# Fifteen products that nobody reads, behind the last product of a two-layer encoder

## The chip, the cores and the metric

The kernel runs on one core of a Trainium2 chip. The metric is the device time of one execution in microseconds (us); less is better. Inputs and outputs lie in the chip's memory, and everything between is one launch.

## The reference

Two encoder layers on 256 tokens of width 1024, all in fp32. In short:

```python
for l in range(2):
    # mixer: one projection to 2560 columns, three groups of attention heads side by side
    proj = rms_norm(x, norm1_g[l]) @ w_in[l]
    out_a = neighbourhood_attention(...)      # 4 heads
    out_d = dilated_window_attention(...)     # 6 heads
    out_c = gqa_block_attention(...)          # 6 heads
    x = x + concat(rms_norm each group) @ w_out[l]
    # feed-forward, 2816 wide
    g, u = split(rms_norm(x, norm2_g[l]) @ w_gate_up[l], 2)
    g = depthwise_conv_centred(g, conv_w[l], conv_b[l])
    x = x + (gelu(g) * u) @ w_down[l]
return x
```

## The kernel before

Tokens stand in two tiles of 128 partitions. Every weight matrix is streamed from memory in units of at most 1 MB (tile `raw`), and each fp32 number is split into two parts, `hi` (rounded to the type fp32r) and `lo` (the rest), on ACT and DVE. A full-precision product is then written as three fp32r products into one accumulator (`mm3`, line 708: hi·hi, hi·lo, lo·hi; lo·lo is left out). Where the profile's names show `wp_hi`, `wp_lo`, `act_ch`, `act_cl` and so on, they are such parts. TensorE's rows show fp32r and fp32 alike as `f32`.

Products into four banks of the tag `psa` hold long sums (projections, the down projection's `dacc`); four more banks of the tag `psw` hold short ones. Products on fp32 data that is not split occur only as transposes, which go through `nc.tensor.transpose` with the 128x128 identity `ident`. Scores of a pair of heads use row halves of the array: the heads' 64 rows lie on partitions 0 to 63 (`LOW`) and 64 to 127 (`HIGH`), and the products alternate between the two halves and write to two banks. At the kernel's start 28 bf16 products on the tile `warm` fill the wait for the first data. No product on column halves (a 64-column stationary operand that writes 64 partitions) occurs.

What is recorded is not what is issued: every call `nc.tensor...` goes through a planner (class `Plan`), which gives each engine's instructions an order from an estimate of times and, among those that could start at the same time, from a rank. `nc.later(n)` adds n to the rank. All instructions are issued at line 472 (1547 is the end of the program: each engine drains there, and all meet at a barrier), so the profile's rows are told apart by tile names, not by lines.

The end of the program is this. The last layer's last down projection (`down(last)`) completes the four quarters of the output (two token tiles by two halves of the columns), which are sums in the four banks of `psa` (`dacc`). For each quarter DVE scales the sum and adds it to the residual `xs` (SCALAR_TENSOR_TENSOR, output `const_x`), and SP writes it out (`out_dram<-const_x`). One quarter is cut in two, and its columns 768 to 1024 are summed in a bank of their own (`end`, of the tag `psw`). The planner puts the quarter of token tile 0 and columns 0 to 512 last, so the program's last eight products, 512 columns wide, go into its bank. The lines for `end`:

```python
nc.vector.scalar_tensor_tensor(xs[:, 1, hs], hold["end"], r2[:, 1:2], xs[:, 1, hs], ALU.mult, ALU.add)
nc.sync.dma_start(ov[:, 1, hs], xs[:, 1, hs])
```

Of the kernel before, what the change touches and what calls it, by code (L numbers as in the profile page):

```python
# [11 lines left out]
F32 = mybir.dt.float32  # L12
# [6 lines left out]
P = 128  # L19
S = 256  # L20
# [3 lines left out]
HD = 64  # L24
# [214 lines left out]
class Plan:  # L239
# [5 lines left out]
    def pool(self, real, name, bufs, space=bass.MemoryType.SB):  # L245
        return PlanPool(self, real, name, bufs, space)
# [271 lines left out]
def encoder_kernel(  # L518
# [21 lines left out]
    nc = Plan(tc)  # L540
# [8 lines left out]
    psw = pool("psw", 4, space=bass.MemoryType.PSUM)  # L549
# [8 lines left out]
    ident = const.tile([P, P], F32, tag="ident", name="ident")  # L558
# [18 lines left out]
    warm = const.tile([P, P], mybir.dt.bfloat16, tag="warm", name="warm")  # L577
# [168 lines left out]
    def mean_squares(name):  # L746

        ss = small.tile([P, NT, 2], F32, tag="ssx", name=f"ssx_{name}", bufs=2)
        for h in range(2):
            for t in range(NT):  # L750
                junk = act.tile([P, 512], F32, tag="s2k", name=f"sq_{name}{t}{h}", bufs=NS2K)
                nc.scalar.activation(
                    junk, xs[:, t, h * 512 : (h + 1) * 512], AF.Square, accum_out=ss[:, t, h : h + 1]
                )
        s1 = small.tile([P, NT], F32, tag="s1x", name=f"s1_{name}", bufs=2)
        nc.gpsimd.tensor_tensor(s1, ss[:, :, 0], ss[:, :, 1], op=ALU.add)
        me = small.tile([P, NT], F32, tag="mex", name=f"me_{name}", bufs=2)
        nc.gpsimd.tensor_scalar(me, s1, 1.0 / D, EPS, ALU.mult, ALU.add)
        r = small.tile([P, NT], F32, tag="rx", name=f"rx_{name}", bufs=2)
        nc.gpsimd.tensor_tensor(r, me, minus_half[:, :NT], op=ALU.pow)  # L760
        return me, r
# [127 lines left out]
    for l in range(DEPTH):  # L889
# [68 lines left out]
        if l == 0:  # L958
# [3 lines left out]
            gq = const.tile([P, DEPTH * 3 * HD], F32, tag="gq", name="gq")  # L962
# [6 lines left out]
            gq = gq.rearrange("p (l a d) -> p l a d", l=DEPTH, d=HD)  # L969
# [359 lines left out]
        _, r2 = mean_squares(f"n2{l}")  # L1329
# [148 lines left out]
        if l == DEPTH - 1:  # L1478
            hs = slice(768, 1024)
            nc.vector.scalar_tensor_tensor(xs[:, 1, hs], hold["end"], r2[:, 1:2], xs[:, 1, hs], ALU.mult, ALU.add)  # L1480
            nc.sync.dma_start(ov[:, 1, hs], xs[:, 1, hs])
    nc.emit()


# [67 lines left out]
```

## Time and profile before

| | |
|---|---|
| median of three runs | 608.33 us (607.88 to 609.16) |
| the profiled execution, first to last instruction (span) | 606.6 us |
| granted TensorE clock | 1.000 |
| PE busy | 600.9 us, 99% of the span, 3496 products |
| DVE busy | 484.9 us, 80% |
| ACT busy | 428.6 us, 71% |
| POOL busy | 80.9 us, 13% |

The page gives no time of the profiled execution beside its span. The median of the runs lies 1.7 us above that span; what lies around the first and the last instruction is in that difference. A product's duration in a row runs to its modelled end and overlaps the next product's; how often products follow each other is read from the differences of their starts.

### The profile page before, as it was taken

The numbers are of one execution on the slowest core, as the hardware profiler recorded it, in microseconds if no ns is written. First come the engines' busy times: TensorE is split into PE (matmuls) and PEld (weight loads), VectorE is DVE, ScalarE is ACT, GpSimd is POOL, SyncE is SP. The second block draws the span as 40 slices with busy tenths as digits, with TensorE's granted clock in tenths as the row PEclk, the third lists the DMA queues.
The fourth block names the chain that finished last, engine by engine and source line by source line (L and its number), as shares of the span: only waits on it lengthen the run. The fifth ranks groups of instructions, "written<-read, shape, count | busy, mean of one in ns | idle before, by whom it ended". The sixth has DMA issues, their size and how long they took to land.

```text
span 606.6 us, 9899 instructions
## 1 busy us (share of the span) xinstructions
PE 600.9 (99%) x3496; PEld 526.7 (87%) x3496; DVE 484.9 (80%) x995; ACT 428.6 (71%) x1065; POOL 80.9 (13%) x130
## 2 busy tenths in 40 slices
PE   8999999999999999999999999999999999999997
PEld 7999898888888888888899989888888888888886
DVE  4899897997788988887777898777977777777775
ACT  6889999686666767666688899676765555665661
POOL 2733030103400000000022214421000000000000
PEclk9999999999999999999999999999999999999999
DMA  8994303566598899988455726844465555555601
GB/s 280 296 294 140 105 36 107 195 202 228 185 224 297 278 342 322 318 304 290 153 147 162 248 70 243 291 163 139 142 205 209 174 175 206 184 166 207 199 9 69
DMA packets 85217, 121.44 MB, mean 200 GB/s; under 512 B 9880, under 2 KB 69880, under 8 KB 85168
## 3 DMA queue, kind: packets, MB, share of 16 engines
q1 hardware_dynamic: 82896, 112.17, 56.3%
q0 software_dynamic: 1728, 8.39, 3.9%
q8 instruction: 27, 0.44, 0.3%
q10 hardware_dynamic: 544, 0.26, 0.2%
q14 instruction: 22, 0.18, 0.1%
HBM read 110.93 MB, written 9.88 MB: 199 GB/s over the span
## 4 chain that ended last, share of the span: by engine, by line
PE 96%; ACT 2%; DVE 1%; POOL 0%; issue 0%; DVEq 0%; ACTq 0%; POOLq 0%
PE psw_w L472 53%; PE psa_a L472 43%; ACT act_s2k L472 1%; ACT wp_hi L472 0%; DVE act_z L472 0%; DVE wp_lo L472 0%; POOL small_rstd L472 0%; ACT act_z L472 0%; ACT act_hT L472 0%; DVE act_sw L472 0%; POOL small_ms L472 0%; DVE const_x L472 0%; DVE act_qo L472 0%; POOL const_warm L472 0%; DVEq L472 0%
## 5 line engine op out<-in xcount | busy, mean ns | idle before, releaser
L472 DVE TENSOR_TENSOR wp_lo<-wp_raw,wp_hi 128x512 fp32r<-128x512 f32 (+2 forms) x332 | 231.5, 731 | 59.1 <-ACT wp_hi L472 39.3
L472 ACT CAST wp_hi<-wp_raw 128x512 fp32r<-128x512 f32 (+2 forms) x332 | 203.0, 663 | 22.8 <-PE psw_w L472 10.2
L472 PE MATMUL psw_w<-act_hT,wp_hi 128*128 128x512 f32 x704 | 180.4, 393 | 0.0
L472 PEld LDWEIGHTS psw_w<-act_hT,wp_hi 128*128 128x128 f32 x704 | 127.8, 189 | 24.8 <-DVE act_hT L472 0.7
L472 PE MATMUL psa_a<-wp_hi,act_hT 128*128 128x384 f32 (+2 forms) x448 | 113.1, 333 | 0.7 <-ACT wp_hi L472 0.7
L472 PEld LDWEIGHTS psw_w<-act_hT,wp_lo 128*128 128x128 f32 x704 | 97.7, 190 | 6.8
L472 PE MATMUL psw_w<-act_hT,wp_lo 128*128 128x256 f32 x704 | 102.2, 282 | 0.0
L472 PEld LDWEIGHTS psa_a<-wp_hi,act_hT 128*128 128x128 f32 x448 | 78.3, 189 | 3.4 <-ACT wp_hi L472 0.9
L472 ACT COPY act_s2k<-psw_w 128x256 f32<-128x256 f32 x88 | 32.4, 373 | 62.2 <-PE psw_w L472 61.9
L472 PE MATMUL psa_a<-wp_lo,act_hT 128*128 128x384 f32 (+2 forms) x224 | 74.4, 334 | 0.1
L472 PE MATMUL psa_a<-wp_lo,act_ch 128*128 128x512 f32 (+1 forms) x176 | 68.9, 392 | 0.0
L472 PE MATMUL psa_a<-wp_hi,act_ch 128*128 128x512 f32 x176 | 68.8, 392 | 0.0
L472 PE MATMUL psa_a<-wp_hi,act_cl 128*128 128x512 f32 (+1 forms) x176 | 68.5, 393 | 0.0
L472 DVE TENSOR_TENSOR act_s2k<-psw_w,act_s2k 128x256 f32<-128x256 f32 x88 | 36.6, 421 | 14.5 <-ACT act_s2k L472 14.1
L472 PEld LDWEIGHTS psa_a<-wp_lo,act_hT 128*128 128x128 f32 x224 | 42.2, 189 | 2.4 <-DVE wp_lo L472 1.0
L472 PEld LDWEIGHTS psa_a<-wp_hi,act_cl 128*128 128x128 f32 x176 | 33.1, 188 | 7.5
L472 PEld LDWEIGHTS psa_a<-wp_hi,act_ch 128*128 128x128 f32 x176 | 33.2, 189 | 6.7
L472 PEld LDWEIGHTS psa_a<-wp_lo,act_ch 128*128 128x128 f32 x176 | 33.1, 188 | 6.7
L472 DVE SCALAR_TENSOR_TENSOR act_s2k<-act_s2k,act_cw,act_s2k 128x255 f32<-128x255 f32 x88 | 36.7, 477 | 1.4 <-ACT act_s2k L472 1.3
L472 ACT ACTIVATE act_s2k<-act_s2k 128x512 f32<-128x512 f32 x22 | 13.9, 631 | 30.2 <-DVE act_s2k L472 30.2
L472 ACT ACTIVATE act_s2k<-act_s2k,act_cw 128x256 f32<-128x256 f32 x44 | 24.1, 595 | 15.3 <-DVE act_s2k L472 15.3
L472 POOL TENSOR_TENSOR small_rstd<-small_ms,const_mh 128x6 f32<-128x6 f32 (+2 forms) x26 | 30.8, 1186 | 14.4 <-DVE small_ms L472 12.8
(132 smaller groups left out, 791.6 us busy)
## 6 DMA issues: line engine op xcount, KB each, us to landing
wp_raw<-in_w_gate_up_dram SPq DMA_DIRECT2D x44, 1024.0 KB, 5.1
wp_raw<-in_w_down_dram SPq DMA_DIRECT2D x22, 1024.0 KB, 7.3
wp_raw<-in_w_in_dram SPq DMA_DIRECT2D x14, 768.0 KB, 6.0
wp_raw<-in_w_in_dram SPq DMA_DIRECT2D x8, 1024.0 KB, 9.1
wp_raw<-in_w_out_dram SPq DMA_DIRECT2D x8, 768.0 KB, 8.4
dram_khi<-act_mixT_hi SPq DMA_DIRECT2D x4, 768.0 KB, 3.6
dram_klo<-act_mixT_lo SPq DMA_DIRECT2D x4, 768.0 KB, 8.3
wp_lo<-dram_klo POOLq DMA_DIRECT2D x4, 768.0 KB, 4.8
```

Source lines behind the costliest of these rows:

```text
L472: getattr(o.engine.real, o.method)(*map(real, o.args), **{k: real(v) for k, v in o.kw.items()})
```

## The change

Behind everything else, 15 products are recorded with `later(100000)`. They read finished data (`gq`, the query gains, as fp32; `ident`; `warm`, bf16) and write to banks of `psw` that nobody reads afterwards: six on column halves, two on the full array, four on row halves, all fp32 and 256 columns wide, and three in bf16, 512 wide.

```diff
+    with nc.later(100000):
+        z = psw.tile([P, 512], F32, tag="w", name="idle0")
+        flat = gq.rearrange("p l a d -> p (l a d)")
+        for _ in range(3):
+            for r in (slice(0, HD), slice(HD, P)):
+                nc.tensor.matmul(z[r, :S], ident[:, r], flat[:, :S], start=True, stop=True)
+        z = psw.tile([P, 512], F32, tag="w", name="idle1")
+        for _ in range(2):
+            nc.tensor.matmul(z[:, :S], ident, flat[:, :S], start=True, stop=True)
+        z = [psw.tile([P, 512], F32, tag="w", name=f"idle{i}") for i in (2, 3)]
+        for _ in range(2):
+            for r, y in zip((slice(0, HD), slice(HD, P)), z):
+                nc.tensor.matmul(y[:, :S], ident[r], flat[r, :S], start=True, stop=True)
+        z = psw.tile([P, 512], F32, tag="w", name="idle4")
+        for _ in range(3):
+            nc.tensor.matmul(
+                z.rearrange("p (a b) -> p a b", b=P), warm, warm.unsqueeze(1).to_broadcast([P, 4, P]),
+                start=True, stop=True,
+            )
     nc.emit()
```

TensorE's instructions at the end of the program, before (-) and now (+); `psa_a_157` is the bank of the quarter that is completed last (`dacc[0][0]`), `psw_w_124`, `117`, `166` and `83` are the four banks of `psw`, and the last of these was `end`:

```order
 L472 MATMUL psa_a_157<-wp_lo_248,act_ch_828 128x512
 L472 MATMUL psa_a_157<-wp_hi_240,act_cl_838 128x512
-L1547 UNCONDITIONAL_BRANCH
+L472 MATMUL psw_w_124<-const_gq_178,const_ident_89 64x256 x6
+L472 MATMUL psw_w_117<-const_gq_178,const_ident_89 128x256 x2
+L472 MATMUL psw_w_166<-const_gq_178,const_ident_89 128x256
+L472 MATMUL psw_w_83<-const_gq_178,const_ident_89 128x256
+L472 MATMUL psw_w_166<-const_gq_178,const_ident_89 128x256
+L472 MATMUL psw_w_83<-const_gq_178,const_ident_89 128x256
+L472 LDWEIGHTS const_warm_77
+L472 MATMUL psw_w_124<-const_warm_77 128x512
+L472 LDWEIGHTS const_warm_77
```

All fifteen stand behind the last product of the computation, ahead of TensorE's end of program; two more pairs of a weight load and a bf16 product follow the last row. No row of another engine moves.

## Prediction

> **What bounds the kernel now.** I read the page first, then the chain of work that ended last, then the last microseconds in order of time, then what each engine does at the end of the program, since that is where the new products go.
>
> ```profile
> span 606.6 us, 9899 instructions
> ...
> PE 600.9 (99%) x3496; PEld 526.7 (87%) x3496; DVE 484.9 (80%) x995; ACT 428.6 (71%) x1065; POOL 80.9 (13%) x130
> ...
> PE 96%; ACT 2%; DVE 1%; POOL 0%; issue 0%; DVEq 0%; ACTq 0%; POOLq 0%
> ```
>
> TensorE bounds the kernel: 99% busy, and 96% of the chain that ended last. Work added to it is paid in full, unless it stands where something else ends later. The chain's last pieces (start, length, what) show that place:
>
> ```profile
> 557.99 11.18 PE psw_w L472 x64
> 569.16 5.58 PE psa_a L472 x24
> ...
> 600.86 1.87 PE psa_a L472 x8
> 602.73 0.02 issue
> 602.75 0.75 DVE const_x L472
> ```
>
> In order of time (the first row is DVE's, the rest run in order):
>
> ```profile
> 600.92 0.48 DVE L472 SCALAR_TENSOR_TENSOR const_x<-psw_w,small_rx,const_x 128x256 f32<-128x256 f32 x1
> ...
> 602.08 0.40 PE L472 MATMUL psa_a<-wp_lo,act_ch 128*128 128x512 f32 x1
> 602.32 0.39 PE L472 MATMUL psa_a<-wp_hi,act_cl 128*128 128x512 f32 x1
> 602.75 0.75 DVE L472 SCALAR_TENSOR_TENSOR const_x<-psa_a,small_rx,const_x 128x512 f32<-128x512 f32 x1 [1.35 <-PE psa_a L472]
> 603.53 0.33 SPq L472 DMA_DIRECT2D out_dram<-const_x  x1
> ```
>
> TensorE's last product ends at 602.71; DVE then works until 603.50, and SP issues the last transfer at 603.53. The span ends 3.9 us after TensorE's end, at 606.6. What fills that time stands under the line of the end of the program (for each engine and operation: count, durations min/median/max in ns, first and last start), and in SP's own waits (in total, times, longest):
>
> ```profile
> L1547 SPq EVENT_SEMAPHORE  x9: 27/28/28, 603.9 to 605.7; - x9
> L1547 SPq DRAIN  x2: 7/10/13, 605.8 to 605.9; - x2
> L1547 POOLq EVENT_SEMAPHORE  x2: 17/17/17, 605.9 to 606.0; - x2
> L1547 PEldq DRAIN  x1: 3227/3227/3227, 599.5 to 599.5; - x1
> L1547 DVEq DRAIN  x1: 789/789/789, 602.8 to 602.8; - x1
> ```
>
> ```profile
> SPq L1547 <- DMA out_dram<-const_x: 1.4, 1, 1.4
> ```
>
> Every engine drains and then meets the others. TensorE's drain is taken up early and ends with its last product: 599.5 + 3.23 = 602.7. DVE's ends at 602.8 + 0.79 = 603.6. SP waits 1.4 us for the last transfer to land and drains at 605.9; only then does POOL pass its first semaphore (605.9), which lets all go on. From there to the end of the span it is another 606.6 - 605.9 = 0.7 us of drains and semaphores. So TensorE has 605.9 - 602.7 = 3.2 us in which it may work for nothing; the ends are rounded to a tenth, and I take 3.1. Beyond that, each microsecond is one of the kernel's time.
>
> **The change part by part.** The forecast is therefore one sum, X, the time from the end of the last real product to the end of the last idle one, less 3.1.
>
> *Waits: nothing.* Four of the five idle banks' readers are long done. The bank `end` is read by DVE's addition of 256 columns, which starts at 600.92 and takes 0.48: over at 601.4, before TensorE is through with the real products at 602.7. Behind an idle product on TensorE stands nothing but its drain. DVE's last addition, SP's last transfer and its landing depend on the real product, which ends at 602.71 as before, so none of them moves. All transfers of weights are over.
>
> *The price of a product.* Rows whose starts show how closely products follow each other: 24 products of 512 columns in 5.58 us, 0.23 each; 64 in 11.18, half of them 512 and half 256 wide, leave (11.18 - 32 x 0.23) / 32 = 0.12 for 256 columns. These are fp32r. For bf16, and for the only products on fp32 data that is not split, the transposes, there are their group's row (mean duration 280 ns) and the rows in order of time:
>
> ```profile
> L472 PE MATMUL psw_w<-const_ident,const_x 128*128 128x128 f32 x64 | 9.7, 280 | 0.0
> ```
>
> ```profile
> 6.57 0.82 PE L472 MATMUL psw_w<-const_warm 128*128 128x256 bf16 x6
> 7.30 0.44 PE L472 MATMUL psa_a<-wp_hi,act_hT 128*128 128x384 f32 x1
> 7.58 0.34 PE L472 MATMUL psa_a<-wp_lo,act_hT 128*128 128x384 f32 x1
> 7.76 0.60 PE L472 MATMUL psw_w<-const_ident,const_x 128*128 128x128 f32 x4
> 8.11 0.60 PE L472 MATMUL psa_a<-wp_hi,act_hT 128*128 128x384 f32 x2
> ```
>
> Six bf16 products of 256 columns, 0.82 with the last one's 0.28 (the duration of 256 columns in the row at 47.45 below): (0.82 - 0.28) / 5 = 0.11, so 0.22 for 512 columns and 3 x 0.22 = 0.66 for the three idle ones. Four transposes of 128 columns: (0.60 - 0.28) / 3 = 0.11, twice the price of fp32r per column, though a transpose's price may be that of its weight load.
>
> The fp32 products, twelve of 256 columns, have no row. In the compiled program each stands as two weight loads and two products; TensorE has 27 products more than before (24 and the three in bf16). Lower bound of one such issued product: that of fp32r, 0.12. Upper bound: an fp32 product made whole from two parts of each operand takes four partial products (the kernel's own split takes three and leaves one out), two for each issued one, so 2 x 0.12, or the row of 512 columns, 0.23. The transposes, the nearest row, say 0.22 for 256 columns. I take 0.23.
>
> [...]
>
> *Halves side by side.* The kernel's scores work on row halves:
>
> ```profile
> 45.22 0.34 PE L472 MATMUL psa_a<-wp_hi,act_hT 128*128 128x384 f32 x1
> 45.48 1.70 PE L472 MATMUL psw_w<-act_ko,act_qo 64*128 64x256 f32 x24
> 47.11 0.50 PE L472 MATMUL psa_a<-wp_hi,act_hT 128*128 128x256 f32 x2
> 47.45 0.28 PE L472 MATMUL psa_a<-wp_lo,act_hT 128*128 128x256 f32 x1
> ```
>
> 24 products in 47.11 - 45.48 = 1.63 us, 0.07 each where a full one of that width takes 0.12: the two halves run at the same time. An idle fp32 product issues its two parts on the same half, one after the other; then come the two of the other half. In order of issue only the second part of one product can run beside the first part of the next. Four products on row halves (8 parts) then take 5 turns, six on column halves (12 parts) take 7. For column halves no row exists; bounds are 7 turns, if they behave as row halves do, and 12, if one follows the other. I take 7, by the row of the row halves, the nearest.
>
> *Changing the form.* The burst holds 12 x 0.12 = 1.40 of work in 1.63, and before it lies 45.48 - 45.22 = 0.26 where a product of 384 columns takes 0.17; after it, the second product follows at 47.11 + 0.50 - 0.28 = 47.33, 0.22 instead of 0.12. Together 0.23 + 0.09 + 0.10 = 0.42 for there and back, 0.2 a change. The idle products change four times (full, columns, full, rows, full): 0.8 us.
>
> *The sum:* column halves 7 x 0.23 = 1.61; full 4 x 0.23 = 0.92; row halves 5 x 0.23 = 1.15; bf16 0.66; changes 0.8. X = 5.14. TensorE's drain would end at 602.7 + 5.1 = 607.9 instead of 602.7, 2.0 after the others are ready. Span 606.6 + 2.0 = 608.6. The median of the runs lies 1.7 above the span, so 608.3 + 2.0 = 610.3, slower by 0.33%. A measurement of this kernel can tell about 0.2%, 1.2 us, from no change; X would have to exceed 3.1 + 1.2 = 4.3 for that.
>
> **The rivals.**
>
> *Column halves in series, row halves side by side.* For it: the trace shows no product on column halves. X = 5.14 + 5 x 0.23 = 6.3, cost 3.2, time 611.5. [...]
>
> *Everything in series.* Were the pairing undone by the two parts that follow each other on one half: another 3 x 0.23, X = 7.0, cost 3.9, time 612.2. Against it: the row halves' burst.
>
> *Not slower: a pass of fp32 costs what fp32r costs.* With 0.12 for each issued product and halves side by side, X = 16 x 0.12 + 0.66 + 0.8 = 3.4, cost 0.3, time 608.6; in series 24 x 0.12 + 1.46 = 4.3, cost 1.2, time 609.5, at the edge. It decides if an issued product takes under (4.3 - 1.46) / 16 = 0.18. For it: no row has a whole fp32 product. Against it: the transposes' 0.22.
>
> [...]
>
> *Nothing happens,* or less: the end of the program doesn't wait for TensorE, or the end moves by other means. The drain that ends with the last product speaks against it. Time 608.3. I see no way to a gain.
>
> **How the numbers follow.** Halves side by side at 0.23: 0.45. Column halves in series: 0.20. All in series: 0.13. Fp32 at the price of fp32r: 0.13. Four passes per issued product: 0.05. Nothing: 0.04. The likeliest gives 610.3; with the first three cases lie 0.78 between 610.3 and 612.2. The range takes these in, with 0.4 for noise above and down to 608.9 for the cheaper fp32 in part: 608.9 to 612.6. Slower by over 0.2% are cases one to three and five: 0.83. Within 0.2% are the cheap fp32, which straddles the edge, and nothing: 0.15. Faster: 0.02, for noise.
>
> **What would show it.** In the changed kernel's trace: TensorE's rows go on after 602.3, in five groups, with 12, 4, 8 and 3 products; starts 0.23 apart on the full array; on row halves some pairs of starts a few ns apart; no idle time before the first. TensorE's drain ends at 607.9 and is the last, so POOL's first semaphore follows it and not SP's drain; SP's wait for the transfer stays 1.4; DVE's last addition stays at 602.75. I am wrong if POOL's semaphore stays at 605.9, if starts on the full array are 0.12 or 0.47 apart, or if a real product starts later than before.

## The result and the profile after

The changed kernel took 609.64 us (median of 13 runs, 609.30 to 610.99) against 608.55 (13 runs, 607.88 to 609.37): ratio 1.0018, 95% interval 1.0009 to 1.0026, so 0.5 to 1.6 us slower. The forecast was 610.3 us and 0.33%: the direction is right, the time lies in the range, and the size is about half.

The profiled execution's span went from 606.6 to 608.7, 2.1 us more. That is one execution against one, and not all of it is the change's. The page's first line, and the end of the chain of work that ended last (start, length, what):

```profile
span 608.7 us, 9954 instructions
```

```profile
569.86 5.58 PE psa_a L472 x24
...
601.56 1.85 PE psa_a L472 x8
603.41 4.33 PE psw_w L472 x27
```

The piece `psa_a x8` is the last real one; before it started at 600.86. The real work ended 0.7 us later in this execution, though nothing ahead of it was changed; an earlier piece, of 24 products, stood 0.7 later already (569.86, before 569.16), and the second profile of before, below, is late by 0.6 too. Behind the last real piece stand 27 products, 4.33 us. Before, the chain went on to DVE there; now TensorE itself ends last. In order of time, with TensorE's weight loads (PEld), whose rows separate the forms (column halves, full array, row halves, bf16):

```profile
603.02 0.39 PE L472 MATMUL psa_a<-wp_hi,act_cl 128*128 128x512 f32 x1
603.34 1.06 PEld L472 LDWEIGHTS psw_w<-const_gq,const_ident 128*64 128x64 f32 x12 [0.37 <-issue]
603.34 3.64 PE L472 MATMUL psw_w<-const_gq,const_ident 128*64 128x256 f32 x24
603.45 0.75 DVE L472 SCALAR_TENSOR_TENSOR const_x<-psa_a,small_rx,const_x 128x512 f32<-128x512 f32 x1 [1.35 <-PE psa_a L472]
...
604.79 0.73 PEld L472 LDWEIGHTS psw_w<-const_gq,const_ident 128*128 128x128 f32 x4 [0.39 <-issue]
605.85 0.73 PEld L472 LDWEIGHTS psw_w<-const_gq,const_ident 64*128 64x128 f32 x8 [0.33 <-issue]
606.91 0.33 PEld L472 LDWEIGHTS <-const_warm 128*128 128x128 bf16 x3 [0.33 <-issue]
606.92 0.82 PE L472 MATMUL psw_w<-const_warm 128*128 128x512 bf16 x3
```

Counts of 12, 4, 8 and 3 are as forecast: two loads and two products for each fp32 product. The groups start 603.34, 604.79, 605.85 and 606.92, and the last product ends at 606.92 + 0.82 = 607.74. DVE's last addition follows its product by the same distance as before (its start 603.45 against 603.02; before 602.75 against 602.32). The end of the program, under its line (1567 here), and SP's waits:

```profile
L1567 SPq EVENT_SEMAPHORE  x12: 17/28/1389, 604.6 to 608.6; - x12
L1567 POOLq EVENT_SEMAPHORE  x4: 17/17/17, 608.0 to 608.6; - x4
L1567 SPq DRAIN  x3: 7/7/13, 607.9 to 608.2; - x3
```

```profile
SPq L1567 <- PE psw_w L472: 1.4, 1, 1.4
SPq L1567 <- DMA out_dram<-const_x: 1.3, 1, 1.3
```

One thing here was not forecast. SP passes one semaphore after another at the end; one of them now is TensorE's own, for which SP waits 1.4 us after it has waited 1.3 for the transfer. Only after that come SP's remaining step and its drain (607.9), and POOL's first semaphore at 608.0. So POOL does not follow TensorE's drain at once, but 0.2 us after TensorE's last product. From the last real product's end (603.41) to POOL's first semaphore it is 4.6 us, before 3.2 (605.9 against 602.7): 1.4 us longer, in agreement with the timed 0.5 to 1.6.

### The profile page after: what moved, and what is told of

Read it like the earlier page. It is cut to its first block, busy times and chain, and to the rows that moved or that the text cites. A ratio compares the mean times of both kernels' runs of the same rounds, so it can differ in the third digit from the quotient of the medians.

```text
span 608.7 us, 9954 instructions
## 1 busy us (share of the span) xinstructions
PE 605.1 (99%) x3523; PEld 528.3 (87%) x3523; DVE 484.9 (80%) x995; ACT 428.3 (70%) x1065; POOL 81.0 (13%) x130
## 4 chain that ended last, share of the span: by engine, by line
PE 96%; DMA 1%; ACT 1%; DVE 1%; POOL 1%; issue 0%; SPq 0%
PE psw_w L472 52%; PE psa_a L472 44%; DMA const_x<-in_x_dram 1%; ACT act_s2k L472 0%; SPq L472 0%; POOL small_rstd L472 0%; POOL small_ms L472 0%; DVE act_z L472 0%; ACT act_hT L472 0%; DVE wp_lo L472 0%; DVE act_sw L472 0%; ACT wp_hi L472 0%; POOL const_gq L472 0%; DVE act_qo L472 0%
```

## The experiments

**A second profile of the kernel before** (no edit).

> The kernel before once more, for a second profile. In the two profiles the last real product ended 0.70 us later in the changed kernel than in the one before, though nothing ahead of it was changed. Theory (it is the variation of one execution to the next, from transfers and POOL's waits in the first 40 us): the last real product ends somewhere between 602.5 and 604 here too, and the end behind it is the same 3.2 us. Rival (the change shifts the earlier work): it ends at 602.7 within 0.1.

One execution, 609.06 us, span 607.3. Its chain and its end:

```profile
601.46 1.87 PE psa_a L472 x8
603.33 0.03 issue
603.36 0.75 DVE const_x L472
```

```profile
L1547 SPq DRAIN  x3: 7/7/13, 606.4 to 606.7; - x3
```

The last real product ends at 603.3, 0.6 later than in the first profile of the same kernel, and SP's first drain follows by 3.1 as it did there. The other profiles with untouched real work have their last piece end at 602.7 to 603.2. So the 0.7 us are the variation of executions. It arises far ahead of the change, and not only in the first 40 us as expected: by the starts of TensorE's products, this profile is 0.1 us behind the first one at 390 us and 0.6 at 399 us, the changed kernel's 0.5 and 0.7. What held TensorE there stays open. Comparisons below go from the last real product's end, or by timed ratios.

**A short tail.** The column and row halves are left out (against the changed kernel):

```diff
-        for _ in range(3):
-            for r in (slice(0, HD), slice(HD, P)):
-                nc.tensor.matmul(z[r, :S], ident[:, r], flat[:, :S], start=True, stop=True)
...
-            for r, y in zip((slice(0, HD), slice(HD, P)), z):
-                nc.tensor.matmul(y[:, :S], ident[r], flat[r, :S], start=True, stop=True)
```

> Only the two full fp32 products and the three in bf16 are left behind the last real product: 4 x 0.22 + 3 x 0.22 = 1.5 us of TensorE's time instead of 4.3. Theory (the end of the program waits for the last landing anyway, so about 3 us behind the last product are free): within 0.1% of before, and POOL's first semaphore again follows SP's drain some 3.2 us after the last real product. Rival (idle products cost wherever they stand, since TensorE bounds the kernel): 1.5 us slower, 0.25%. Rival (any idle product at the end makes SP wait for TensorE's own semaphore and so lengthens the end): 0.1 to 0.3 us slower even here.

Ratio 1.0001 (0.9992 to 1.0010). In its chain and under its end of program (line 1559):

```profile
603.20 1.51 PE psw_w L472 x7
```

```profile
L1559 SPq EVENT_SEMAPHORE  x12: 17/28/28, 604.4 to 607.1; - x12
L1559 POOLq EVENT_SEMAPHORE  x4: 17/17/17, 606.4 to 607.0; - x4
```

1.51 us of products cost nothing that the times can tell: POOL's first semaphore comes 606.4 - 603.2 = 3.2 after the real work, as before. That rules out that an idle product costs wherever it stands (0.25%). The smaller lengthening of 0.1 to 0.3 us is too small for the times, but the profile speaks against it: none of SP's steps takes over 28 ns, where one took 1389 in the changed kernel, so TensorE's semaphore is met before SP comes to it.

**Twice as many products of each form.** The four loops run 6, 4, 4 and 6 times:

```diff
-        for _ in range(3):
+        for _ in range(6):
             for r in (slice(0, HD), slice(HD, P)):
...
```

> The same five groups, each with twice as many products, and still four changes of form: TensorE's time behind the last real product is 2 x 3.67 + 0.65 = 8.0 us. Theory (free up to 3.0, then one for one): cost 8.0 - 3.0 = 5.0 us against before, 0.83%; starts stay 0.22 apart. Rival (the cost is mostly in the changes of form, or a fixed one of having idle products): 1 to 2 us, 0.2 to 0.3%. Rival (everything paid): 8.0 us, 1.3%.

Ratio 1.0092 (1.0078 to 1.0106), 4.7 to 6.4 us. Chain, and the starts of the forms:

```profile
603.06 7.99 PE psw_w L472 x54
```

```profile
602.99 2.36 PEld L472 LDWEIGHTS psw_w<-const_gq,const_ident 128*64 128x64 f32 x24 [0.36 <-issue]
...
605.73 1.59 PEld L472 LDWEIGHTS psw_w<-const_gq,const_ident 128*128 128x128 f32 x8 [0.38 <-issue]
607.66 1.60 PEld L472 LDWEIGHTS psw_w<-const_gq,const_ident 64*128 64x128 f32 x16 [0.33 <-issue]
609.58 0.98 PEld L472 LDWEIGHTS <-const_warm 128*128 128x128 bf16 x6 [0.33 <-issue]
```

7.99 - 3.0 = 5.0: beyond the free stretch it is one for one, and neither everything nor a fixed sum is paid. The differences between this kernel and the changed one price each form without its change: full array 1.93 against 1.06, 0.87 for four parts more, 0.22 each; columns 2.74 against 1.45, 1.29 for 12 parts more; rows 1.92 against 1.06, 0.86 for eight. So two parts on halves take one turn of 0.22 (a turn is the time of one issued part). What is left of each group is the change of form: 0.16, 0.19, 0.20, and 0.09 ahead of the first product (603.34 - 603.02 - 0.23), 0.64 in all.

**The same products ahead of the real ones.**

```diff
-    with nc.later(100000):
+    with nc.later(-100000):
```

> The same fifteen products with a rank that puts them ahead of the last 36 or so real products instead of behind the last one; some of those real products change places among themselves. Theory: here nothing covers them, so all of their 4.3 us are paid, 0.7%, and DVE's last addition is 4.3 us later against the start of the last down projection, while the end of the program behind the last real product is as long as before (3.2 us to POOL's first semaphore). Rival (the place makes no difference): 1.1 to 1.4 us, 0.2%, as behind the last product.

The idle products now stand among the last down projection's. Ratio 1.0076 (1.0061 to 1.0092), 3.7 to 5.6 us, which takes in all of the 4.3 us: three to four times what the same products cost behind the last one. The idle products begin at 596.32, and the chain behind them ends thus:

```profile
596.32 3.64 PE L472 MATMUL psw_w<-const_gq,const_ident 128*64 128x256 f32 x24
...
599.90 0.82 PE L472 MATMUL psw_w<-const_warm 128*128 128x512 bf16 x3
```

```profile
569.51 5.58 PE psa_a L472 x24
...
605.52 1.87 PE psa_a L472 x8
607.39 0.03 issue
607.42 0.75 DVE const_x L472
```

DVE's last addition starts at 607.42 instead of 602.75 or, in the second profile of before, 603.36: 4.1 to 4.7 later. Counted from the same piece of 24 products (569.51 here, 569.16 before), it is 37.91 us and was 33.59: 4.3 later. POOL's first semaphore, at 610.6, again comes 3.2 us behind the last real product, at 607.4. The place decides.

**Only one half of each kind.** Products stay as many, but none has another half to run beside:

```diff
-            for r in (slice(0, HD), slice(HD, P)):
+            for r in (slice(0, HD), slice(0, HD)):
...
-            for r, y in zip((slice(0, HD), slice(HD, P)), z):
+            for r, y in zip((slice(0, HD), slice(0, HD)), z):
```

> All six column-half products use columns 0 to 63, and all four row-half products rows 0 to 63, so that no product finds another half to run beside. In the changed kernel the 12 issued parts on column halves took 6 turns of 0.22 and the 8 on row halves took 4. Theory (a part on one half runs beside a part on the other): now 12 and 8 turns, 10 x 0.22 = 2.2 us more than with the halves alternating, so 2.2 us slower than the changed kernel, 3.3 to 3.6 slower than before. Rival (the two parts of one fp32 product run beside each other on the same half): 6 and 4 turns as in the changed kernel, 1.1 to 1.4 us slower than before.

Ratio 1.0055 (1.0037 to 1.0074), 2.3 to 4.5 us; the idle products take 6.47 us behind the real work:

```profile
602.62 2.35 PEld L472 LDWEIGHTS psw_w<-const_gq,const_ident 128*64 128x64 f32 x12 [0.37 <-issue]
...
605.35 0.73 PEld L472 LDWEIGHTS psw_w<-const_gq,const_ident 128*128 128x128 f32 x4 [0.39 <-issue]
606.41 1.59 PEld L472 LDWEIGHTS psw_w<-const_gq,const_ident 64*128 64x128 f32 x8 [0.33 <-issue]
608.33 0.33 PEld L472 LDWEIGHTS <-const_warm 128*128 128x128 bf16 x3 [0.33 <-issue]
```

Columns take 2.73, less 0.16 for the change 2.57: 12 turns. Rows 1.92 less 0.20: 8 turns. So the two parts of one product did not run beside each other here; in the changed kernel, with 12 parts in 1.29 and 8 in 0.86, it was the two halves that did.

**Halves in blocks.** The order of the loops is turned round: three products on the left column half, then three on the right; two on the low row half, then two on the high one.

```diff
-        for _ in range(3):
-            for r in (slice(0, HD), slice(HD, P)):
+        for r in (slice(0, HD), slice(HD, P)):
+            for _ in range(3):
...
```

> The same products, with the halves in blocks: three on the left column half, then three on the right; two on the low row half, then two on the high one. Theory (TensorE starts products in the order of issue, and a part runs beside the other half's only if they are neighbours): 11 turns instead of 6 for the columns and 7 instead of 4 for the rows, 8 x 0.22 = 1.8 us more than the changed kernel, about 3 us slower than before. Rival (each half has its own order, so that the second block catches up with the first): 6 and 4 turns again, 1.1 to 1.4 us slower than before. The changed kernel speaks for something between: its products alternate by pairs of parts, and 6 turns were possible only if a part went ahead of one that was issued before it.

Ratio 1.0033 (1.0020 to 1.0046), 1.2 to 2.8 us; 4.81 us behind the real work. Neither theory gave that for the columns:

```profile
603.03 1.54 PEld L472 LDWEIGHTS psw_w<-const_gq,const_ident 128*64 128x64 f32 x12 [0.37 <-issue]
...
604.96 0.73 PEld L472 LDWEIGHTS psw_w<-const_gq,const_ident 128*128 128x128 f32 x4 [0.38 <-issue]
606.02 0.74 PEld L472 LDWEIGHTS psw_w<-const_gq,const_ident 64*128 64x128 f32 x8 [0.33 <-issue]
607.09 0.33 PEld L472 LDWEIGHTS <-const_warm 128*128 128x128 bf16 x3 [0.33 <-issue]
```

Columns 1.93 less 0.16: 8 turns, not 11 and not 6. Rows 1.07 less 0.20: 4 turns, as the rival had it, though the order of issue would give 7. One weight load shows it by itself: the fifth part of the rows in order of issue, the first on the high half, goes into the bank that was `end`, and its load carries the wait for DVE's semaphore. In the trace it starts at 606.035, 13 ns after the first part's load (606.022) and ahead of the second part's (606.130). So the second half got ahead of the order of issue here: the rows by 3 turns, all that there was to gain, the columns by 3 of 5.

**Longer blocks.** Six and six products on column halves, four and four on row halves (against the kernel with the blocks):

```diff
         for r in (slice(0, HD), slice(HD, P)):
-            for _ in range(3):
+            for _ in range(6):
...
         for r, y in zip((slice(0, HD), slice(HD, P)), z):
-            for _ in range(2):
+            for _ in range(4):
```

> As the blocks before, but each block twice as long: six fp32 products on the left column half, then six on the right (12 and 12 issued parts), four on the low row half, then four on the high one (8 and 8). In the shorter blocks the right half's first part, the seventh in order of issue, started with the left half's third, and the high half's first, the fifth, with the low half's first: each time four places ahead. Theory (the halves have orders of their own, but TensorE looks only about four parts ahead): the right half starts with the left one's ninth part, 8 + 12 = 20 turns; the high half with the low one's fifth, 4 + 8 = 12 turns. TensorE's time behind the last real product is then (20 + 4 + 12 + 3) x 0.216 + 0.65 = 9.1 us and the cost against before 9.1 - 3.0 = 6.1 us, 1.0%. Rival (no limit of that kind; in the shorter blocks the start was late for another reason): columns 14 turns as late as there by two, rows 8: 6.9 us, cost 3.9. Rival (strictly in order of issue): 23 and 15 turns, 10.4 us, cost 7.4.

Ratio 1.0086 (1.0069 to 1.0103), 4.2 to 6.3 us; 9.23 us behind the real work, 0.1 off the theory of four places; the costs of both rivals, 3.9 and 7.4, lie outside the interval:

```profile
603.01 4.13 PEld L472 LDWEIGHTS psw_w<-const_gq,const_ident 128*64 128x64 f32 x24 [0.37 <-issue]
...
607.53 0.73 PEld L472 LDWEIGHTS psw_w<-const_gq,const_ident 128*128 128x128 f32 x4 [0.39 <-issue]
608.59 2.56 PEld L472 LDWEIGHTS psw_w<-const_gq,const_ident 64*128 64x128 f32 x16 [0.33 <-issue]
611.49 0.33 PEld L472 LDWEIGHTS <-const_warm 128*128 128x128 bf16 x3 [0.33 <-issue]
```

Columns 4.52 less 0.16 is 20 turns, rows 2.90 less 0.20 is 12 and a half; strictly by the order of issue they would be 23 and 15, without a limit 14 and 8. In the trace the thirteenth part of the columns starts at 604.797, 6 ns behind the ninth, and the ninth of the rows at 609.566, 6 ns behind the fifth; that high half's second part then follows by 0.32 us instead of 0.22, which is the half turn more. The distance of four places was measured with these two lengths of block alone; what sets it no run shows.

All kernels with idle products at the end, by what stands behind the real work, less the free 3.0:

| | behind the real work, us | less 3.0 | timed, us (95%) |
|---|---|---|---|
| short tail | 1.51 | nothing | -0.5 to 0.6 |
| the change | 4.33 | 1.3 | 0.5 to 1.6 |
| blocks | 4.81 | 1.8 | 1.2 to 2.8 |
| one half | 6.47 | 3.5 | 2.3 to 4.5 |
| twice | 7.99 | 5.0 | 4.7 to 6.4 |
| long blocks | 9.23 | 6.2 | 4.2 to 6.3 |

## Why the prediction was right, and where its size was off

*The mechanism stood.* The new work is free until the other engines reach the end of the program, and one for one beyond: shown by the short tail at one end, by twice the products at the other, and by the same products ahead of the real ones, where nothing is free. Waits cost nothing, as forecast: the first idle product starts at 603.34, 0.32 behind the start of the last real one, which is its 0.23 and 0.09 for the change of form.

*The free stretch* was taken as 3.1 and is 3.0: 3.2 to POOL's first semaphore, less the 0.2 from TensorE's last product to POOL's first semaphore. The prediction had nothing but TensorE's drain behind an idle product, and that drain releasing POOL directly; the trace has SP waiting 1.4 us for TensorE's semaphore, and POOL follows SP's drain as before (608.0 behind 607.9; before both at 605.9), so this sign of the prediction did not come.

*X was 4.33 and not 5.14*, and this is the step that failed. Term by term: column halves 6 turns of 0.22, 1.29 instead of 1.61; row halves 4 turns, 0.86 instead of 1.15; full array 0.87 instead of 0.92; bf16 about as forecast (0.66); changes of form 0.64 instead of 0.8. The largest part is the number of turns: the prediction let parts start in the order of issue, and in the trace the other half's part went ahead. The 12 parts of the columns start in six pairs, the two of a pair 6 to 7 ns apart. On the rows the load that carries the wait for DVE's semaphore, the third in order of issue, starts at 605.855, 6 ns behind the first (605.849) and ahead of the second (605.957). The rival of column halves in series falls, for they ran as the row halves did, and the rival of everything in series falls with it.

*The price of fp32* was right: an issued part of 256 columns takes 0.22 (on the full array starts at 605.11, 605.33 and 605.54), the transposes' price by column, not 0.12. X and the time alone could not have told that: the rival of fp32 at the price of fp32r, in series, had X = 4.3 and 609.5 us, nearly what was measured. It falls by the full array, where four parts more take 0.87, and by the experiment with one half, where series cost 2.1 us more than halves side by side (6.47 against 4.33). The two parts of a product take 0.43, four times the 0.11 of 256 bf16 columns. Column halves ran at the row halves' pace, 0.22 for a pair. No run shows the 0.47 for an issued part, which stands among the prediction's signs and had 0.05 of the chances as four passes per issued product; the runs show 0.22.

*The chances:* 0.83 went to slower by over 0.2%. By the median it is 0.18%, just inside the class that had 0.15, by the interval 0.09 to 0.26%. X came out at the 4.3 that the prediction named as the point from which a difference could be told, so its overestimate of X moved the outcome onto that edge. That the time lies in the range is in part luck: the stretch of the range below 610.3 was there for a cheaper fp32, which did not come, and what filled it was fewer turns and cheaper changes of form.

## What to carry to other kernels

An engine that isn't the last to finish can have a free stretch at the end of the program: here TensorE's is set by the last transfer's landing and reaches 3.0 us behind its own last product, and the same 4.3 us of work cost 1.3 behind that product and 4.3 ahead of it, by the profiles. Other engines were not tried. Read the stretch from when each engine drains and who comes last, and look whether the new work adds a semaphore to a queue that passes them one by one, as SP's did here (1.3 us for the transfer, then 1.4 for TensorE's own). Before two profiles' spans are compared, find where the added work begins in each: of a 2.1 us difference in span here, 0.7 was one execution against another.

## What the runs showed of the hardware that was not expected

Products on different halves of the array did not start in the order of issue: with six parts on one half issued ahead of six on the other, the columns took 8 turns where the order allows 11, with twelve and twelve 20 where it allows 23, and with four and four the rows took 4 where it allows 7. In both lengths of block the second half's first part started beside one issued four places ahead of it, in the longer ones 6 ns behind it. With alternating halves the order of the two parts within a product cost nothing: 12 parts took 6 turns of 0.22.
